# Middle stage of a hybrid decoder layer: low weight parts by accumulating transfers inside SBUF, and two more weight slots

## The chip, the cores and the metric

The kernel runs on one core of one Trainium2 chip, in float32 throughout. The metric is the device time of one execution in microseconds (us); three executions of the kernel before have a median of 1206.13 us.

## What is computed

One decoder layer for 512 prompt tokens and 32 sample tokens (8 sequences of 4), 544 columns in all, with the same weights:

```python
x = x + 0.5 * SwiGLU_1(RMSNorm(x))            # D_MODEL 1024, D_FF 2816
h = RMSNorm(x); z = h @ w_in                  # 1024 x 3584, split among head groups
x = x + concat(MoBA(q_a, k_a, v_a),           # 8 heads of 64, softmax attention
               gate * norm(HGRN2(q_b, f_b, i_b))) @ w_out   # 4 heads of 128, gated recurrence
x = x + 0.5 * SwiGLU_2(RMSNorm(x))
```

The prompt attends within itself; the samples attend to 1024 cached keys and values that are gathered by a page table (64 gathers of 512 KB). New keys, values and recurrent states are outputs too.

## The kernel before, in words

**Tiles and products.** Activations lie transposed, features on the 128 partitions and 544 tokens along the free dimension. A float32 product is made of three TensorE passes in float32r: weights and activations are each cut into a high part (the value rounded to float32r) and a low part (the rest), and high x high, high x low and low x high are added in PSUM (`products`, line 608). One output tile of a projection takes 8 row blocks x 2 column halves x 3 passes = 48 matmuls of 272 columns.

**Weights.** A weight matrix is worked off in jobs (`weight_jobs`, line 449), each of two "units" of up to 128x512 elements (256 KB). A unit is loaded by SyncE into one of four `raw` buffers (`w_load`), then split (`split_unit`, line 530): ScalarE copies it with rounding into `whi`, VectorE subtracts that from the raw tile into `wlo`. The pair lies in one of four weight slots (line 993). A projection takes two units (`next_w(2)` in `gemm`, line 618) and gives them back at its end (`free_w`), which calls `w_pump` (line 572): as long as fewer than AHEAD = 4 units are waiting, and a slot is free, the next unit is split; then as many loads are issued as raw buffers allow. With four slots and two in use, two units can lie ready ahead. The two FFNs use Strassen-like paired jobs for most of gate and up, which borrow six further slots; gate and up of the first five blocks, down, w_in and w_out are plain jobs.

**Stages.** FFN 1 (about 0 to 400 us); the mixer or middle stage (about 400 to 790 us: 28 projections from w_in, the attention of prompt and samples, the recurrence, two products with w_out); the other six products with w_out and FFN 2 (to the end). In the middle stage the projections are the backbone of TensorE's order, and chains of other work are woven into it: `pair_qk` (line 1142) norms a pair of key and query heads, with the tiles `kn` (high part by ScalarE, low part by VectorE), `qh`, `ql`, and a multiply of `kt` on GpSimd; `prompt_tile` does one tile of the prompt's softmax attention; `hgrn_head` one head of the recurrence; `sample_scores` and `sample_rest` read the gathered cache, tiles `KV`, five buffers. The chain of a sample's values (`sample_rest`) can begin only when all four value projections are done.

**What sets the order.** A planner (`Order`, line 254) runs the whole program once with modelled costs for each engine and for the DMA engines, and notes each instruction with its modelled start; the instructions are then given out in the order of these starts, so every engine's queue is fixed by the model. TensorE goes on with a due chain if there is one, and with the backbone otherwise. For a transfer the model takes 0.06 us of the issuing engine, 1.5 us of latency and the bytes at 330 KB a us (`Order.dma`, line 358); 1.0 us of GpSimd for an indirect gather. GpSimd issues the gathers and, at the end of the stage, eight reloads of x (`y<-xs`, line 1769). The queue of each engine is strictly in order: an instruction that waits holds back all behind it.

Before, line 534 is the only thing that makes a low part:

```python
hi, lo = self.take_slot(x, (F32R, F32R))
nc.scalar.copy(hi[:, :nk], src[:, :nk])
nc.vector.tensor_tensor(lo[:, :nk], src[:, :nk], hi[:, :nk].bitcast(F32), op=ALU.subtract)
```

Of the kernel before, what the change touches and what calls it, by code (L numbers as in the profile page):

```python
# [14 lines left out]
AF = mybir.ActivationFunctionType  # L15
ALU = mybir.AluOpType
# [5 lines left out]
KD = D // 128  # L22
# [19 lines left out]
COLS = {"qa": 0, "ka": 512, "va": 1024, "qb": 1536, "fb": 2048, "ib": 2560, "gb": 3072}  # L42
# [8 lines left out]
OVER, TICK, WARM_COLUMNS = 0.0112, 3.413, 3060  # L51
NREG = 5
AHEAD = 4
PACE = 0.8
WARM = 10
SLACK = -0.1
# [52 lines left out]
class View:  # L109
# [9 lines left out]
    def step(self, op, *args, **kw):  # L119
        return View(self.tensor, getattr(self.model, op)(*args, **kw), self.path + ((op, args, kw),))  # L120
# [58 lines left out]
class Engine:  # L179
# [22 lines left out]
    def __getattr__(self, op):  # L202
        real = getattr(self.real, op)

        def call(*args, **kw):
            names = list(self.tensors(args, kw))
            if op == "dma_start":
                s = self.order.dma(self.part, 4 * args[1].shape[0] * self.free(args[1]), names)
            elif op == "indirect_dma_start":
                s = self.order.dma(self.part, 4 * args[0].shape[0] * self.free(args[0]),  # L210
                                   names + [args[3].ap.tensor.name], 1.0)
            else:
                s = self.order.spend(self.part, self.cost(op, args, kw), names, op, self.shares_port(op, args, kw))
            self.order.note(s, real, args, kw)

        return call
# [37 lines left out]
class Order:  # L254
# [100 lines left out]
        for n in names:  # L355
            self.touched[n] = max(done, self.touched.get(n, 0.0))

    def dma(self, part, size, names, cost=0.06):
        s = self.fit(part, self.start(part, names), cost)
        e = self.fit("dma", s + cost + 1.5, size / 330e3) + size / 330e3  # L360
        self.finish(names, e, e + 0.3)
        return s

# [49 lines left out]
class Build:  # L413
# [35 lines left out]
    def weight_jobs(self):  # L449
        a, out = self.a, []  # L450

        def quarters(m, nk, r0, c0):
            h = nk // 2
            return [m[128 * r:128 * (r + h), c0:c0 + 128].rearrange("(k p) m -> p k m", p=128)
                    for r in (r0, r0 + h)]

        def plain(m, nk, r0, c0):
            out.append({"paired": False, "src": quarters(m, nk, r0, c0), "nk": nk // 2, "raw": [], "done": 0})

        def ffn(p):  # L460
            gate, up, down = (a[p + n][0] for n in ("_gate", "_up", "_down"))
            for g0, ng in FGROUPS:
                for f in range(g0, g0 + ng):
                    if f < NREG:
                        plain(gate, KD, 0, 128 * f)
                        plain(up, KD, 0, 128 * f)
                    else:
                        out.append({"paired": True, "nk": KD // 2, "raw": [], "done": 0,
                                    "src": quarters(gate, KD, 0, 128 * f) + quarters(up, KD, 0, 128 * f)})
                for m in range(KD):  # L470
                    plain(down, ng, g0, 128 * m)

        ffn("ffn1")
        for n, j in IN_ORDER:
            plain(a["w_in"][0], KD, 0, COLS[n] + 128 * j)
        for m in range(KD):
            plain(a["w_out"][0], KD, 0, 128 * m)
        ffn("ffn2")
        return out

# [46 lines left out]
            self.loading += 1  # L527
        return True

    def split_unit(self, src, nk, x):  # L530
        nc = self.nc
        hi, lo = self.take_slot(x, (F32R, F32R))
        nc.scalar.copy(hi[:, :nk], src[:, :nk])
        nc.vector.tensor_tensor(lo[:, :nk], src[:, :nk], hi[:, :nk].bitcast(F32), op=ALU.subtract)
        return hi, lo, x

    def w_split(self):
        if self.splitting == len(self.jobs):
            return False
        job = self.jobs[self.splitting]  # L540
        n = job["done"]
        if len(job["raw"]) <= (3 if job["paired"] else n):
            return False
        x = self.room("w", job)
        if x is None:
            return False
        nk = job["nk"]
        if job["paired"]:
            (a11, a12, a21, a22) = (r for r, _ in job["raw"])
            if n == 0:  # L550
                S = [self.tl(self.sums, [128, 4, 128], f"S{i}") for i in range(4)]
                for i, (e, p, q, op) in enumerate(((self.nc.vector, a21, a22, ALU.add),
                                                   (self.nc.vector, S[0], a11, ALU.subtract),
                                                   (self.nc.gpsimd, a11, a21, ALU.subtract),
                                                   (self.nc.gpsimd, a12, S[1], ALU.subtract))):
                    e.tensor_tensor(S[i][:, :nk], p[:, :nk], q[:, :nk], op=op)
                job["units"] = (a11, S[1], S[0], a12, S[2], S[3], a22)
            src = job["units"][n]
            self.units.append(self.split_unit(src, nk, x))
            drop = {0: (0, 2), 3: (1,), 6: (3,)}.get(n, ())  # L560
        else:
            self.units.append(self.split_unit(job["raw"][n][0], nk, x))
            drop = (n,)
        for i in drop:
            raw, y = job["raw"][i]
            self.release(y, raw)
        job["done"] += 1
        if job["done"] == (7 if job["paired"] else 2):
            self.splitting += 1
        return True  # L570

    def w_pump(self):
        while (len(self.units) < AHEAD and self.w_split()) or self.w_load():
            pass

    def next_w(self, n):
# [84 lines left out]
    def right_factors(self, pool, x, gain):  # L661
# [14 lines left out]
        for k in range(n):  # L676
# [12 lines left out]
            for step in steps:  # L689
                step()  # L690
                self.order.t = self.order.free["pe"] + PACE
                yield
# [278 lines left out]
    def load_x(self, pool, p, x):  # L971

        nc, a = self.nc, self.a
# [3 lines left out]
        s = p.tile([NS, D], F32, name="xins")  # L977
        nc.scalar.dma_start(s, a["x_sample"].rearrange("b t d -> (b t) d"))
        xin = {}
        src = a["x_prompt"][0].rearrange("(i p) d -> p i d", p=128)  # L980

        def load(c, n):
            t = p.tile([128, 4, n], F32, name=f"xin{c}")
            nc.sync.dma_start(t, src[:, :, c:c + n])
            for k in range(n // 128):
# [4 lines left out]
        self.units = []  # L990
        self.turn = False
        self.slots = {"raw": [{"pool": self.wp, "tags": ("raw",), "bufs": 4, "used": 0, "freed": [], "extra": None}],
                      "w": [{"pool": self.wp, "tags": ("whi", "wlo"), "bufs": 4, "used": 0, "freed": [], "extra": None}]}
        w = [self.first_weights() for _ in range(2)]
        load(0, 128)
        w[0][1](0)
# [50 lines left out]
        out = [self.tl(pool, [128, T], t, bufs=2) for t in ("t_s", "t_h")]  # L1047
# [797 lines left out]
```

## Time and profile before

| | |
|---|---|
| Median of three executions | 1206.13 us (1203.18 to 1208.79) |
| The profiled execution | 1210.65 us, its span 1208.9 us |
| TensorE busy | 1178.1 us, 97% of the span |
| VectorE, ScalarE, GpSimd busy | 858.5, 551.9, 228.3 us |
| Bytes moved | 144.74 MB, 120 GB/s on the mean |

How to read the rows further down. PE is TensorE's matmuls, PEld its weight loads, DVE VectorE, ACT ScalarE, POOL GpSimd, SPq the queue of SyncE. Every instruction of this kernel is recorded at line 284, where the planner gives it out, so the tiles' names tell the operations apart: `wlo<-raw,whi` reads raw and whi and writes wlo. A row of a table by stretches has the stretch in us, its length, busy us of PE, PEld, DVE, ACT and POOL (number of instructions in brackets), then the mean granted clock of TensorE (1.00 is 2.4 GHz, 0.50 is 1.2 GHz), the mean busy share of the 16 DMA engines, and GB/s. A row of a timeline has the start, the length, the engine, the operation and the tiles, the number of instructions merged into it, and in square brackets the idle time before it and what ended it. A row of groups has the count, the busy us and mean ns of one, then the idle time before them and what ended it. A row of waits says who waited for whom: us in total, times, the longest.

### The profile page before, as it was taken

Reading aid. Unit: us, or ns where it says so; the run is one execution under the profiler, and the core shown is the slowest. Engines: PE = TensorE matmul, PEld = TensorE weight load, DVE = VectorE, ACT = ScalarE, POOL = GpSimd, SP = SyncE. Lnnn points to the kernel's source line nnn. Section 1 sums busy time; section 2 is a strip of 40 time slices with the busy share of each in tenths; the row PEclk is TensorE's granted clock in tenths of the full one; section 3 lists DMA queues with packets and bytes.
Section 4 is the critical chain, followed back from the end, with each engine's and each line's share of the span. In section 5 each row is a group of like instructions: output and inputs, shape, how many; then the busy total and the mean of one; then the engine's idle time right before and its main releaser. Section 6 shows DMA issues by size and latency. Waiting matters only on the chain.

```text
span 1208.9 us, 26320 instructions
## 1 busy us (share of the span) xinstructions
PE 1178.1 (97%) x10571; PEld 1113.7 (92%) x10571; DVE 858.5 (71%) x1729; ACT 551.9 (46%) x1125; POOL 228.3 (19%) x211
## 2 busy tenths in 40 slices
PE   8999999999999999989999999899999999999998
PEld 8989999999999988878878867799999999999998
DVE  6988559954875698877776557667977488736843
ACT  6455246532654345554556433344554266524632
POOL 3012012200202401000332344220020023102200
PEclk9999999999999999989999999899999999999999
DMA  5244453333314642322565776352344323323222
GB/s 161 79 123 114 133 148 97 97 106 87 87 54 135 193 129 69 97 72 74 181 195 160 235 262 222 111 158 79 93 118 131 97 81 104 106 87 88 63 79 82
DMA packets 216238, 144.74 MB, mean 120 GB/s; under 512 B 12035, under 2 KB 204067, under 8 KB 216116
## 3 DMA queue, kind: packets, MB, share of 16 engines
q1 hardware_dynamic: 205588, 106.60, 30.6%
q0 software_dynamic: 10432, 36.32, 9.1%
q8 instruction: 83, 1.36, 0.5%
q14 instruction: 39, 0.32, 0.1%
q10 hardware_dynamic: 96, 0.14, 0.0%
HBM read 133.94 MB, written 11.83 MB: 121 GB/s over the span
## 4 chain that ended last, share of the span: by engine, by line
PE 77%; DVE 13%; ACT 3%; DMA 3%; issue 2%; SPq 1%; POOL 0%; DVEq 0%; ACTq 0%; POOLq 0%
PE mm L284 51%; PE sm L284 26%; DVE wlo L284 3%; DVE xl L284 2%; DVE xwl L284 1%; DMA raw<-ffn_down 1%; ACT xh L284 1%; DVE t_h L284 1%; SPq L284 1%; ACT whi L284 1%; DVE hl L284 1%; ACT sq L284 1%; DMA raw<-ffn_up 1%; DVE S L284 1%; DMA KV<-cache_v,idx 1%
## 5 line engine op out<-in xcount | busy, mean ns | idle before, releaser
L284 PE MATMUL mm<-xh,whi 128*128 128x272 f32 x1216 | 365.0, 300 | 1.0 <-DVE t_g L284 0.5
L284 PE MATMUL mm<-xl,whi 128*128 128x272 f32 x1216 | 352.4, 290 | 5.4 <-DVE xl L284 5.2
L284 PE MATMUL mm<-xh,wlo 128*128 128x272 f32 x1216 | 353.2, 290 | 1.1 <-DVE wlo L284 1.1
L284 ACT CAST whi<-raw 128x512 fp32r<-128x512 f32 (+1 forms) x230 | 138.7, 604 | 261.4 <-PE mm L284 192.3
L284 PEld LDWEIGHTS mm<-xh,whi 128*128 128x128 f32 x1216 | 231.5, 190 | 18.2 <-issue 15.7
L284 PEld LDWEIGHTS mm<-xl,whi 128*128 128x128 f32 x1216 | 231.3, 190 | 6.4 <-DVE xl L284 6.2
L284 PEld LDWEIGHTS mm<-xh,wlo 128*128 128x128 f32 x1216 | 231.0, 190 | 2.1 <-DVE wlo L284 2.1
L284 DVE TENSOR_TENSOR wlo<-raw,whi 128x512 fp32r<-128x512 f32 (+1 forms) x230 | 165.1, 727 | 81.0 <-ACT whi L284 77.4
L284 POOL TENSOR_TENSOR S<-raw,raw 128x512 f32<-128x512 f32 x18 | 30.4, 1691 | 380.9 <-DMA raw<-ffn_up 261.1
L284 PE MATMUL mm<-hh,whi 128*128 128x272 f32 x352 | 101.5, 288 | 0.3 <-DVE x L284 0.3
L284 PE MATMUL mm<-hh,wlo 128*128 128x272 f32 x352 | 101.1, 287 | 0.0
L284 PE MATMUL mm<-hl,whi 128*128 128x272 f32 x352 | 101.1, 287 | 0.0
L284 PE MATMUL mm<-xwh,xh 128*128 128x272 f32 x296 | 85.4, 288 | 1.3 <-DVE t_h L284 0.8
L284 PE MATMUL sm<-xwl,xh 128*128 128x272 f32 x296 | 85.3, 288 | 0.0
L284 PE MATMUL mm<-xwl,xh 128*128 128x272 f32 x296 | 85.3, 288 | 0.0
L284 PE MATMUL sm<-xwh,xh 128*128 128x272 f32 x296 | 85.2, 288 | 0.0
L284 PE MATMUL mm<-xwh,xl 128*128 128x272 f32 x296 | 85.2, 288 | 0.0
L284 PE MATMUL sm<-xwh,xl 128*128 128x272 f32 x296 | 85.2, 288 | 0.0
L284 DVE TENSOR_TENSOR xl<-S,xh 128x512 fp32r<-128x512 f32 x84 | 66.0, 796 | 4.1 <-ACT xh L284 3.7
L284 PEld LDWEIGHTS mm<-hh,whi 128*128 128x128 f32 x352 | 66.3, 188 | 0.7 <-ACT whi L284 0.5
L284 ACT CAST xh<-S 128x512 fp32r<-128x512 f32 x84 | 51.8, 620 | 32.7 <-DVE S L284 13.7
L284 PEld LDWEIGHTS mm<-hh,wlo 128*128 128x128 f32 x352 | 66.2, 188 | 0.0
(325 smaller groups left out, 2639.2 us busy)
## 6 DMA issues: line engine op xcount, KB each, us to landing
raw<-ffn_down SPq DMA_DIRECT2D x64, 256.0 KB
raw<-ffn_gate SPq DMA_DIRECT2D x56, 256.0 KB
raw<-ffn_up SPq DMA_DIRECT2D x56, 256.0 KB
raw<-w_in SPq DMA_DIRECT2D x56, 256.0 KB
raw<-ffn_down SPq DMA_DIRECT2D x32, 192.0 KB
xl<-ffn_gate SPq DMA_DIRECT2D x16, 256.0 KB
xh<-ffn_up SPq DMA_DIRECT2D x16, 256.0 KB
xl<-ffn_up SPq DMA_DIRECT2D x16, 256.0 KB
```

The source lines that it names most:

```text
L284: call(*map(real, args), **{k: real(v) for k, v in kw.items()})
```

## The change

For the jobs of w_in and w_out alone (marked "mixer"), VectorE's subtraction is replaced: ScalarE writes the negated, rounded copy of the raw tile into the low tile, and GpSimd issues a transfer inside SBUF that adds the raw tile onto it. For these jobs up to AHEAD_MIX = 6 units are split ahead instead of 4. The weight slots are six instead of four in every stage; the room for them comes from a descriptor scratch of 8192 bytes a partition. The planner takes 1.3 us of GpSimd for each direct transfer that it issues, the reloads of x too, and 3.0 us of latency for an accumulating one.

```diff
+AHEAD_MIX = 6
             if op == "dma_start":
-                s = self.order.dma(self.part, 4 * args[1].shape[0] * self.free(args[1]), names)
+                pool = self.part == "pool"
+                s = self.order.dma(self.part, 4 * args[1].shape[0] * self.free(args[1]), names,
+                                   1.3 if pool else 0.06, 3.0 if "accum_op" in kw else 1.5)
-    def dma(self, part, size, names, cost=0.06):
+    def dma(self, part, size, names, cost=0.06, latency=1.5):
         s = self.fit(part, self.start(part, names), cost)
-        e = self.fit("dma", s + cost + 1.5, size / 330e3) + size / 330e3
+        e = self.fit("dma", s + cost + latency, size / 330e3) + size / 330e3
         for n, j in IN_ORDER:
-            plain(a["w_in"][0], KD, 0, COLS[n] + 128 * j)
+            plain(a["w_in"][0], KD, 0, COLS[n] + 128 * j, True)
         for m in range(KD):
-            plain(a["w_out"][0], KD, 0, 128 * m)
+            plain(a["w_out"][0], KD, 0, 128 * m, True)
-    def split_unit(self, src, nk, x):
+    def split_unit(self, src, nk, x, transfer=False):
         nc = self.nc
         hi, lo = self.take_slot(x, (F32R, F32R))
         nc.scalar.copy(hi[:, :nk], src[:, :nk])
+        if transfer:
+            nc.scalar.activation(lo[:, :nk], src[:, :nk], AF.Identity, scale=-1.0)
+            nc.gpsimd.dma_start(lo[:, :nk], src[:, :nk], accum_op=ALU.add)
+            return hi, lo, x
         nc.vector.tensor_tensor(lo[:, :nk], src[:, :nk], hi[:, :nk].bitcast(F32), op=ALU.subtract)
         return hi, lo, x
-            self.units.append(self.split_unit(job["raw"][n][0], nk, x))
+            self.units.append(self.split_unit(job["raw"][n][0], nk, x, job["mixer"]))
     def w_pump(self):
-        while (len(self.units) < AHEAD and self.w_split()) or self.w_load():
+        def ahead():
+            mixer = self.splitting < len(self.jobs) and self.jobs[self.splitting]["mixer"]
+            return len(self.units) < (AHEAD_MIX if mixer else AHEAD)
+
+        while (ahead() and self.w_split()) or self.w_load():
             pass
-                      "w": [{"pool": self.wp, "tags": ("whi", "wlo"), "bufs": 4, "used": 0, "freed": [], "extra": None}]}
+                      "w": [{"pool": self.wp, "tags": ("whi", "wlo"), "bufs": 6, "used": 0, "freed": [], "extra": None}]}
-    nc = bacc.Bacc("TRN2", target_bir_lowering=False, num_devices=1)
+    nc = bacc.Bacc("TRN2", target_bir_lowering=False, num_devices=1, dynamic_dma_scratch_size=8192)
```

## Rows read from the trace of the kernel before

**Rows 1.** The page: span, and busy time and share of each engine.
```profile
span 1208.9 us, 26320 instructions
PE 1178.1 (97%) x10571; PEld 1113.7 (92%) x10571; DVE 858.5 (71%) x1729; ACT 551.9 (46%) x1125; POOL 228.3 (19%) x211
```

**Rows 2.** Table by stretches: plain products, and the stage of the prompt's attention.
```profile
410.00:420.00 10.00, 10.00 (x82) 10.00 (x81) 3.70 (x7) 3.04 (x6) 7.19 (x12) 1.00 0.68 191
430.00:560.00 130.00, 124.78 (x998) 108.43 (x1000) 108.54 (x282) 65.21 (x158) 9.41 (x9) 0.95 0.29 83
```

**Rows 3.** Table by stretches: the two places at which the clock fell.
```profile
495.00:505.00 10.00, 9.34 (x52) 8.09 (x51) 8.74 (x23) 5.23 (x13) 0.87 (x1) 0.83 0.29 82
530.00:545.00 15.00, 11.98 (x53) 9.71 (x53) 10.83 (x30) 6.51 (x18) 0.04 (x1) 0.66 0.25 70
```

**Rows 4.** Table by stretches: the value gathers, and the end of the mixer.
```profile
700.00:728.00 28.00, 27.35 (x406) 18.97 (x407) 15.53 (x42) 8.46 (x24) 15.19 (x16) 1.00 0.78 270
738.00:762.00 24.00, 21.74 (x424) 15.33 (x416) 14.85 (x41) 4.08 (x12) 14.59 (x14) 1.00 0.77 254
762.00:780.00 18.00, 12.51 (x132) 10.97 (x128) 13.47 (x37) 6.48 (x20) 0.00 (x0) 0.81 0.18 55
```

**Rows 5.** Timeline of VectorE: pairs of low-part splits, and the steps of kn.
```profile
448.40 1.28 DVE L284 TENSOR_TENSOR wlo<-raw,whi 128x512 fp32r<-128x512 f32 x2
...
493.76 2.65 DVE L284 TENSOR_TENSOR wlo<-raw,whi 128x512 fp32r<-128x512 f32 x2
...
496.45 0.75 DVE L284 SCALAR_TENSOR_TENSOR kn<-sm,qkg,kn 64x512 fp32r<-64x512 f32 x1
...
527.95 2.65 DVE L284 TENSOR_TENSOR wlo<-raw,whi 128x512 fp32r<-128x512 f32 x2
...
530.62 0.74 DVE L284 SCALAR_TENSOR_TENSOR kn<-sm,qkg,kn 64x512 fp32r<-64x512 f32 x1
```

**Rows 6.** Timeline of ScalarE: its steps of kn ahead of those.
```profile
493.75 0.68 ACT L284 ACTIVATE kn<-sm,qkg 64x512 fp32r<-64x512 f32 x1 [0.69 <-PE sm L284]
...
528.07 0.68 ACT L284 ACTIVATE kn<-sm,qkg 64x512 fp32r<-64x512 f32 x1 [0.92 <-PE sm L284]
```

**Rows 7.** Timeline of GpSimd at the same two times.
```profile
493.96 1.91 POOL L284 TENSOR_TENSOR kt<-kt,gkrow 128x640 f32<-128x640 f32 x1 [23.44 <-issue]
528.28 1.77 POOL L284 TENSOR_TENSOR kt<-kt,gkrow 128x640 f32<-128x640 f32 x1 [32.41 <-PE sm L284]
```

**Rows 8.** TensorE's waits from 440 to 560 us.
```profile
PE sm L284 <- DVE kn L284: 4.1, 3, 3.2
```

**Rows 9.** Groups of VectorE from 400 to 790 us: the low-part splits.
```profile
L284 DVE TENSOR_TENSOR wlo<-raw,whi 128x512 fp32r<-128x512 f32 x60 | 45.1, 768 | 14.7 <-ACT whi L284 14.1
```

**Rows 10.** Timeline of VectorE in the tail of the mixer: one split.
```profile
765.09 0.69 DVE L284 TENSOR_TENSOR wlo<-raw,whi 128x512 fp32r<-128x512 f32 x1
```

**Rows 11.** TensorE's waits over the whole span: those for low parts.
```profile
PE mm L284 <- DVE wlo L284: 1.1, 2, 0.6
```

**Rows 12.** Groups of ScalarE from 400 to 790 us: the high parts, and a scaled copy.
```profile
L284 ACT CAST whi<-raw 128x512 fp32r<-128x512 f32 x60 | 37.1, 619 | 55.6 <-PE mm L284 45.6 <-issue 6.9 <-PE sm L284 1.8
...
L284 ACT ACTIVATE qn<-z,qkg 128x544 f32<-128x544 f32 x4 | 3.0, 755 | 0.5 <-DVE z L284 0.5
```

**Rows 13.** Groups of GpSimd over the span: an indirect and a direct transfer.
```profile
L284 POOL DMA_INDIRECT KV<-cache_v,idx x32 | 31.5, 984 | 43.5 <-PE sm L284 40.0 <-issue 1.2 <-PE mm L284 0.8
...
L284 POOL DMA_DIRECT2D y<-xs x8 | 4.4, 580 | 22.2 <-PE mm L284 22.2
```

**Rows 14.** GpSimd's waits from 690 to 770 us.
```profile
POOL KV L284 <- PE sm L284: 37.8, 23, 11.2
```

**Rows 15.** The page's DMA queues: packets, MB, share of 16 engines.
```profile
q0 software_dynamic: 10432, 36.32, 9.1%
```

**Rows 16.** Timelines of GpSimd and VectorE: the reloads of x and their first use.
```profile
782.70 4.39 POOL L284 DMA_DIRECT2D y<-xs  x8 [22.20 <-PE mm L284]
...
788.43 0.79 DVE L284 TENSOR_TENSOR y<-mm,y 128x272 f32<-128x272 f32 x2 [0.23 <-DMA y<-xs]
```

More of the change, by code (lines that the diff above doesn't have):

```diff
@@ L455, in quarters, with plain @@
                     for r in (r0, r0 + h)]
-        def plain(m, nk, r0, c0):
-            out.append({"paired": False, "src": quarters(m, nk, r0, c0), "nk": nk // 2, "raw": [], "done": 0})
+        def plain(m, nk, r0, c0, mixer=False):
+            out.append({"paired": False, "src": quarters(m, nk, r0, c0), "nk": nk // 2, "raw": [], "done": 0,
+                        "mixer": mixer})
         def ffn(p):
@@ L467, in ffn @@
                     else:
-                        out.append({"paired": True, "nk": KD // 2, "raw": [], "done": 0,
+                        out.append({"paired": True, "nk": KD // 2, "raw": [], "done": 0, "mixer": False,
                                     "src": quarters(gate, KD, 0, 128 * f) + quarters(up, KD, 0, 128 * f)})
```

## The prediction, made before the changed kernel was run

> **What bounds the kernel now.** First the busy shares [rows 1]: TensorE is busy 1178.1 of 1208.9 us, so all that any change of the weight splits can give back is some 31 us of TensorE idle time and the time in which its clock is halved. Then the table by stretches: where is TensorE not full? In a stretch of plain products it starts 82 matmuls in 10 us, 0.122 us each. From 430 to 560 us, the stage of the prompt's attention, it is idle 5.2 of 130 us while VectorE is busy 108.5 [rows 2]. Most of that is two places [rows 3]. From 495 to 505 us TensorE is idle 0.66 us and the granted clock is 0.83: after the pause it ran 3.4 us at 1.2 GHz, 1.7 us of lost work. From 530 to 545 us it is idle 3.02 us at a clock of 0.66: 10.2 us at 1.2 GHz, 7.2 of them busy, 3.6 us lost. So the two places cost 2.4 and 6.6 us. A third is the end of the mixer, 762 to 780 us: 5.5 us idle at a clock of 0.81 [rows 4].
>
> What ends the wait? The timelines of VectorE and ScalarE say it [rows 5, 6]. Both times a pair of key heads is being normed: ScalarE finishes the high part kn at 494.43 and 528.75 us, but VectorE takes up its step of kn only at 496.45 and 530.62, because two low-part splits (wlo, 2.65 us together) stand in front of it. Both pairs run beside GpSimd's kt multiply [rows 7]; a pair without it took 1.28 us [rows 5]. TensorE's products of kn come after that: 4.1 us of waits, one of 3.2 [rows 8]. So VectorE's queue, and the weight splits in it, set the end here, and they are what the change takes away.
>
> **The change part by part.** (1) *VectorE loses its part of 72 units* (56 of w_in, 16 of w_out; 60 of them between 400 and 790 us, 768 ns each, 45.1 us [rows 9]). Most of that lies beside a full TensorE and is worth nothing. On the path are: the first stall, where kn moves up by 496.45 - 494.43 = 2.0 us, more than the 0.66 us of idle time, so the idle time and the fall of the clock go: 2.4 us. The second stall, where kn moves up by 1.87 us: 1.2 us of idle time stays, since further ScalarE and VectorE steps of the same chain follow, and I let half of the clock's loss stay with it: 1.87 + 1.8 = 3.7 us (between 1.9, if the clock falls all the same, and 6.6). The other 1.5 us of idle time from 430 to 560 (5.2 - 0.66 - 3.02): taken by half, 0.7 us (0 to 1.5). In the tail one wlo of 0.69 us stands between the steps of a root that the last head needs [rows 10]: 0.7 us. What is late next in the two stalls is the turn-taking of ScalarE and VectorE on one tile.
>
> (2) *Two more slots, everywhere.* In the two FFNs the limit stays four units, but with six slots two more can be split while two are in use. TensorE's waits for wlo there are 1.1 us in all [rows 11]: I take them whole, 1.1 us (0 to 1.1).
>
> (3) *ScalarE gets the negated copy*: 72 instructions that the trace does not show. Nearest rows: the cast of the same tile, 619 ns, and an activation with a scale on 128x544, 755 ns, or 710 at 512 columns [rows 12]. So 72 x 0.62 to 0.71 = 45 to 51 us on an engine that was busy 552 of 1209 us [rows 1]. Before kn it waited 0.69 and 0.92 us for TensorE [rows 6], so one more copy in front fits there. But some will stand ahead of a softmax or norm step: I charge 1.0 us (0 to 4, if six of them lie bare).
>
> (4) *GpSimd issues 72 transfers*, not in the trace. Nearest: a direct load took 580 ns (4.4 us for eight), an indirect gather 984 [rows 13]: 42 to 71 us on an engine busy for 228. A transfer waits in GpSimd's queue for its negated copy; behind it stand the cache gathers and the kt and state multiplies. The reverse holds too: a transfer can stand behind a gather that waits for a buffer, up to 11.2 us [rows 14]. The cover is GpSimd's idle time and the lead (6).
>
> (5) *72 x 256 KB through the DMA engines.* The software queue moved 36.32 MB in 9.1% of the span [rows 15], 110 us of all 16 engines, 330 KB a us, so 0.79 us a unit; if the target is read as well, 1.6 us. I take 0.79, the nearest row, and keep both ends. In most of the stage this is covered. The place where it may not be is the value gathers, 700 to 728 and 738 to 762 us, with DMA shares of 0.78 and 0.77 [rows 4]: room for 6.2 + 5.5 us. I expect six to eight units between 700 and 780 us; at 0.79 us they need 6.3 us at most, and fit, but a gather in whose way one stands lands later: 1.5 us (0 to 13, see B).
>
> The Trainium skill (DMA: Bandwidth & Descriptors, Rules for kernel authors) says that an accumulating transfer reads its destination and writes it later, and (same page, Issuing engines are not separate DMA queues) that the transfers of all issuers interleave on the same 16 engines. By that I estimate 1.6 us a unit, and the sum below would be some 1 to 5 us worse. No row here shows an accumulating transfer.
>
> (6) *The low part comes later.* Before: a cast, then 0.7 us. After: cast 0.62, negated copy 0.7, issue 0.6, landing. For the landing the nearest row is the first of eight reloads of x: issued at 782.70 us, used at 788.43 after a wait for it [rows 16]: 5.7 us with seven others behind it; from below the 0.8 of the data alone. So 3 to 8 us from raw to low part. The lead is now two projections, four units beside the two in use: 2 x 48 matmuls x 0.122 us = 11.7 us (before 5.9). It covers this, unless the transfer stands behind a gather of 11.2 us. Cost 0.
>
> (7) *The planner* hands out every queue's order by modelled times. It now sees VectorE freer, transfers from GpSimd at 1.3 us and landings of 3.0 us, so TensorE's own order in the middle stage changes. The same products are issued; which stall comes where is not in the trace. I put 0, and 4 us to either side.
>
> Sum: gained 2.4 + 3.7 + 0.7 + 0.7 + 1.1 = 8.6; paid 1.0 + 1.5 = 2.5; net 6.1 us. The profiled execution took 1210.65 us (span 1208.9), so it would become 1204.5. The median of the runs shown is 4.5 us lower, 1206.13, and no term depends on that difference: **1200.0 us**, 0.5% faster.
>
> **The rivals.** *A: the wait moves, the end does not (no change).* VectorE is relieved, but the chain of a pair is then held by ScalarE, which has one more instruction for each unit, and by the turns between the engines. For it: the steps of kn go from ScalarE to VectorE and back. Then only the bare idle time of the stalls comes back, 0.66 + 1.87 = 2.5 us, less 1.0 for ScalarE: 1.5 us, **1204.6**. Against it: from 430 to 560 us ScalarE is busy 65 us against VectorE's 108.5 [rows 2]; 23 units at 0.65 bring it to 80.
>
> *B: the value gathers wait (slower).* From 700 us on the gathers and TensorE's use of five buffers run as one chain, and the end of the mixer hangs on its last buffer. If a unit costs this chain its issue (0.6 to 1.0) and 1.6 us of DMA, 2.4 us, eight units cost 19.2 us; less the 7.6 us that the other terms give (8.6 - 1.0), the kernel is 11.6 us slower: **1217.7**. It decides from about 1.0 us a unit on the chain (8 units = 7.6 us) and is over 0.5% slower from 1.7. For it: from 762 us TensorE has little else to do [rows 4]. Against it: the DMA room of 11.7 us. A second road to the same side: a transfer caught behind an 11.2 us gather wait arrives after 11.2 + 5 us against a lead of 11.7; 4.5 us of idle time, and as much again by the clock. Twice is 18 us, less the 6.1: 1218.
>
> *C: the change gives more.* The whole 9.0 us of the two stalls and 5.5 us of the tail go, since chains that no longer queue on VectorE all end sooner: 1206.1 - 14.5 + 2.5 = **1194**.
>
> **How the numbers follow.** Forecast 0.29 and C 0.13 (the faster side, 0.42); A 0.35; B 0.23. About 0.5%, 6.0 us, is what a measurement of this kernel can tell from no change: faster is below 1200.1, slower above 1212.2. Faster 0.42, same 0.35, slower 0.23. The forecast's own range is 1195 to 1204 (the second stall at its ends, the planner's 4 us in part). The range for 8 in 10 takes in A and C with 2 us beyond, and of B what lies below 1213: **1192 to 1213**.
>
> **What would show it.** Right: no wlo on VectorE from 400 to 790 us; VectorE from 430 to 560 us down from 108 by some 18 us; TensorE's waits for kn (4.1 us) below 2; no stretch of the middle at a clock near 0.5. A: these waits as long, with ScalarE named. B: from 700 us gathers spaced wider, TensorE waiting for KV, a longer tail, or TensorE waiting for wlo with a DMA as releaser. An issue far from 0.6 to 1.0 us on GpSimd, or landings over 8 us, would make steps 4 to 6 wrong.

## The result and the profile after

The changed kernel took 1216.47 us (median; 1213.94 to 1218.02), the kernel before on the same chip 1205.22 us (1203.18 to 1208.79): a ratio of 1.0087, 95% interval 1.0065 to 1.0110. It is slower, by some 11 us, where 6 us less was forecast, and above the range. Run once more on another chip (after_again, below) the same kernel gave 1.0101.

The profiled execution took 1213.94 us, its span is 1212.2 us. It is the fastest of its five, and the profiled execution of before, 1210.65 us, lies above all the times listed for that kernel, so the two profiles differ by 3.3 us only. The second profiled execution of the changed kernel has a span of 1218.4 us, near its median. Both are used.

The page of the changed kernel: busy times, the software queue (packets, MB, share of 16 engines), the new issues with their time to landing, and their group (count, busy us and mean ns, idle time before).

```profile
span 1212.2 us, 26433 instructions
PE 1176.2 (97%) x10571; PEld 1112.8 (92%) x10571; DVE 804.1 (66%) x1657; ACT 588.5 (49%) x1197; POOL 295.1 (24%) x283
...
q0 software_dynamic: 20800, 55.19, 18.0%
...
wlo<-raw POOLq DMA_DIRECT2D x72, 256.0 KB, 4.7
...
L287 POOL DMA_DIRECT2D wlo<-raw x72 | 65.4, 943 | 137.0 <-ACT wlo L287 132.2
```

VectorE gave up 54 us and GpSimd took 67 more than in [rows 1]. The software queue went from 9.1% [rows 15] to 18.0%: 18.0% of 1212.2 less 9.1% of 1208.9 is 108 us, 1.50 us of all 16 engines for each of the 72 units.

The stretches of [rows 2 to 4] again, and the end of the mixer in steps of 5 us (busy PE, PEld, DVE, ACT, POOL; clock; DMA share; GB/s):

```profile
430.00:560.00 130.00, 125.63 (x1159) 109.68 (x1158) 102.86 (x283) 78.97 (x185) 40.11 (x48) 0.99 0.69 161
495.00:505.00 10.00, 10.00 (x82) 9.66 (x81) 9.03 (x26) 8.39 (x15) 3.57 (x4) 1.00 0.91 205
530.00:545.00 15.00, 14.45 (x108) 12.06 (x107) 10.74 (x31) 9.23 (x22) 4.18 (x4) 1.00 0.53 123
738.00:762.00 24.00, 24.00 (x500) 18.70 (x500) 17.32 (x45) 10.71 (x32) 17.79 (x17) 1.00 0.95 285
762.00:780.00 18.00, 13.50 (x125) 11.55 (x125) 11.15 (x31) 4.29 (x7) 0.00 (x0) 0.91 0.30 96
785.00:790.00 5.00, 1.20 (x10) 0.98 (x8) 0.00 (x0) 0.00 (x0) 4.47 (x8) 0.93 1.06 247
790.00:795.00 5.00, 2.46 (x11) 2.46 (x12) 2.02 (x5) 1.30 (x2) 0.54 (x1) 0.50 0.96 330
```

The last two of these stretches in the kernel before:

```profile
785.00:790.00 5.00, 5.00 (x43) 5.00 (x42) 2.31 (x5) 1.87 (x3) 2.09 (x4) 1.00 1.05 342
790.00:795.00 5.00, 5.00 (x42) 5.00 (x41) 3.55 (x7) 3.85 (x8) 1.41 (x1) 1.00 0.89 273
```

The two stalls of [rows 3] are gone: TensorE is full or nearly so, at a clock of 1.00. The value gathers, where rival B put its price, run beside a full TensorE (738 to 762). But from 785 to 795 us, where it was full before, TensorE is idle for 6.3 of 10 us, and then at half its clock. And over the whole stretch from 430 to 560 us it is idle 4.4 us against 5.2 before: a new stall has come, the wait of 3.3 us for hqh in the next rows. What TensorE waited for, over the whole span:

```profile
PE mm L287 <- DVE y L287: 6.9, 2, 6.3
PE mm L287 <- DVE xl L287: 4.7, 4, 3.0
PE sm L287 <- DVE hqh L287: 3.3, 1, 3.3
PE mm L287 <- DVE wlo L287: 2.1, 4, 1.2
```

The 4.1 us of waits for kn [rows 8] are no longer among them. The longest wait is new: for y, the first addition onto the reloaded x. GpSimd's and VectorE's timelines show why:

```profile
780.04 0.99 POOL L287 DMA_DIRECT2D wlo<-raw  x1 [18.40 <-ACT wlo L287]
...
784.83 0.85 POOL L287 DMA_DIRECT2D wlo<-raw  x1 [0.19 <-issue]
786.11 3.79 POOL L287 DMA_DIRECT2D y<-xs  x7 [0.43 <-issue]
790.53 0.54 POOL L287 DMA_DIRECT2D y<-xs  x1 [0.64 <-DMA wlo<-raw]
...
792.04 0.79 DVE L287 TENSOR_TENSOR y<-mm,y 128x272 f32<-128x272 f32 x2 [15.13 <-DMA y<-xs]
```

Four transfers of w_out's units stand in front of the reloads, and the first three of them waited for ScalarE's negated copy (18.40, 0.52 and 1.35 us). ScalarE in its turn stood waiting for TensorE in front of these splits. The first seven reloads then wait for nothing else ("issue" ends the idle time before them), the eighth for the landing of a transfer. Before, they were issued at 782.70 us, when TensorE released them, and used at 788.43 [rows 16].

The second new wait, for xl, is 27 us into the kernel, in FFN 1, which the change was not meant to touch. VectorE's timeline and the table's row for 20 to 30 us, first in the kernel before, then in the changed one:

```profile
20.39 3.09 DVE L284 SCALAR_TENSOR_TENSOR xl<-x,gains,xh 128x544 fp32r<-128x544 f32 x2
26.82 1.29 DVE L284 TENSOR_TENSOR wlo<-raw,whi 128x512 fp32r<-128x512 f32 x2
...
35.72 0.69 DVE L284 COPY R<-sm 128x512 f32<-128x512 f32 x1 [0.68 <-PE sm L284]
...
20.00:30.00 10.00, 10.00 (x81) 10.00 (x81) 7.30 (x10) 5.78 (x11) 6.01 (x5) 1.00 0.12 33
```

```profile
20.70 1.29 DVE L287 SCALAR_TENSOR_TENSOR xl<-x,gains,xh 128x544 fp32r<-128x544 f32 x1
21.91 3.60 DVE L287 TENSOR_TENSOR wlo<-raw,whi 128x512 fp32r<-128x512 f32 x2
25.44 1.85 DVE L287 SCALAR_TENSOR_TENSOR xl<-x,gains,xh 128x544 fp32r<-128x544 f32 x1
...
39.69 0.69 DVE L287 COPY R<-sm 128x512 f32<-128x512 f32 x1 [1.31 <-PE sm L287]
...
20.00:30.00 10.00, 6.99 (x49) 6.77 (x48) 7.98 (x8) 5.75 (x12) 6.56 (x5) 0.91 0.18 52
```

The two extra slots are free at the start, so two more units are split at once, and their 3.60 us on VectorE stand in front of an xl for which TensorE waits 3.0 us. By the copy of R, a later step, the changed kernel is 4.0 us behind; the rest of what FFN 1 loses comes after it and was not traced to a place.

**Where the time lies.** Five segments of the span, read from timelines: FFN 1, up to the first copy of a w_in projection out of PSUM; the prompt's attention, up to the first transposition of a gathered key; the cache, up to the last product with gathered values; the turn, up to the first addition onto the reloaded x; the rest. Microseconds, one profiled execution each.

| kernel | FFN 1 | attention | cache | turn | rest | span |
|---|---|---|---|---|---|---|
| before | 408.1 | 165.1 | 192.3 | 22.9 | 420.5 | 1208.9 |
| after, first | 415.3 | 157.5 | 194.3 | 24.9 | 420.2 | 1212.2 |
| after, second | 416.5 | 161.8 | 195.0 | 24.9 | 420.2 | 1218.4 |
| slots6_alone | 412.8 | 161.5 | 192.4 | 21.3 | 418.2 | 1206.2 |
| four_in_ffn | 408.1 | 160.4 | 196.8 | 25.6 | 420.8 | 1211.7 |
| no_transfer | 414.4 | 154.5 | 196.8 | 14.0 | 423.3 | 1203.0 |
| all_small | 414.6 | 158.0 | 195.6 | 23.6 | 420.6 | 1212.4 |
| out_small | 415.4 | 158.8 | 197.0 | 23.0 | 420.4 | 1214.6 |
| reload_sync | 415.4 | 159.2 | 198.3 | 27.1 | 420.2 | 1220.1 |
| reload_act | 413.6 | 160.2 | 194.7 | 21.4 | 426.0 | 1215.9 |
| w_in_only | 413.8 | 159.9 | 192.7 | 22.9 | 418.9 | 1208.2 |
| w_in_four | 409.0 | 157.3 | 196.9 | 21.3 | 418.9 | 1203.4 |
| w_in_four, again | 409.2 | 160.0 | 194.5 | 21.4 | 419.0 | 1204.1 |
| lead_four | 408.0 | 161.0 | 192.0 | 21.8 | 419.8 | 1202.6 |

The two executions of one and the same kernel differ by 4.3 us in the attention, so a difference of that size between two rows says nothing there. Up to the first splits of the mixer's weights, some 20 us before the end of FFN 1, every engine's queue is in the same order in all kernels with six slots there, and their nine executions take 412.8 to 416.5 us; the five with four slots take 408.0 to 409.2. The rows also come from several chips, on which the medians of the kernel before run from 1205.22 to 1210.19 us: spans are not compared across rows, only stages, and times by ratio. Against before, the changed kernel loses 7.2 to 8.4 us in FFN 1, 2.0 to 2.7 in the cache stage and 2.0 in the turn, and gains 3.3 to 7.6 in the attention.

### The profile page after: what moved, and what is told of

Its sections match the earlier page's. It is cut to its first block, busy times and chain, and to the rows that moved or that the text cites. A ratio compares the mean times of both kernels' runs of the same rounds, so it can differ in the third digit from the quotient of the medians.

```text
span 1212.2 us, 26433 instructions
## 1 busy us (share of the span) xinstructions
PE 1176.2 (97%) x10571; PEld 1112.8 (92%) x10571; DVE 804.1 (66%) x1657; ACT 588.5 (49%) x1197; POOL 295.1 (24%) x283
## 4 chain that ended last, share of the span: by engine, by line
PE 75%; DVE 8%; DMA 6%; issue 5%; ACT 3%; POOL 3%; SPq 0%; POOLq 0%; ACTq 0%; DVEq 0%
PE mm L287 50%; PE sm L287 25%; DMA KV<-cache_v,idx 2%; DVE xl L287 2%; POOL KV L287 1%; DVE wlo L287 1%; DMA raw<-w_in 1%; DVE xwl L287 1%; DMA raw<-ffn_gate 1%; DMA raw<-ffn_up 1%; ACT whi L287 1%; DMA SC<-rsample 1%; DMA xin<-x_prompt 1%; POOL wlo L287 1%; DVE S L287 0%
## 5 line engine op out<-in xcount | busy, mean ns | idle before, releaser
L287 PEld LDWEIGHTS mm<-xh,whi 128*128 128x128 f32 x1216 | 231.3, 190 | 26.8 <-issue 14.7
L287 DVE TENSOR_TENSOR wlo<-raw,whi 128x512 fp32r<-128x512 f32 (+1 forms) x160 | 111.8, 706 | 46.0 <-ACT whi L287 43.2
L287 POOL TENSOR_TENSOR S<-raw,raw 128x512 f32<-128x512 f32 x18 | 27.4, 1522 | 341.2 <-DMA raw<-ffn_up 210.3
L287 POOL DMA_DIRECT2D wlo<-raw x72 | 65.4, 943 | 137.0 <-ACT wlo L287 132.2
L287 PE MATMUL mm<-xwh,xh 128*128 128x272 f32 x260 | 75.5, 290 | 1.9 <-DVE t_h L287 1.3
L287 PE MATMUL sm<-xwh,xl 128*128 128x272 f32 x260 | 75.0, 288 | 0.0
L287 PE MATMUL mm<-xwl,xh 128*128 128x272 f32 x260 | 75.0, 288 | 0.0
L287 PE MATMUL sm<-xwh,xh 128*128 128x272 f32 x260 | 75.0, 288 | 0.0
L287 PE MATMUL mm<-xwh,xl 128*128 128x272 f32 x260 | 75.0, 288 | 0.0
L287 PE MATMUL sm<-xwl,xh 128*128 128x272 f32 x260 | 74.9, 288 | 0.0
L287 PEld LDWEIGHTS mm<-hl,whi 128*128 128x128 f32 x352 | 66.2, 188 | 0.0
## 6 DMA issues: line engine op xcount, KB each, us to landing
raw<-ffn_down SPq DMA_DIRECT2D x32, 192.0 KB, 2.5
```

Source lines behind the costliest of these rows:

```text
L287: call(*map(real, args), **{k: real(v) for k, v in kw.items()})
```

## The experiments

All ratios are to the kernel before on the same chip, with a 95% interval. Diffs are against the changed kernel where nothing else is said.

### Which part of the change costs

**slots6_alone**: the kernel before with six slots and the scratch.

```diff
-  "tags": ("whi", "wlo"), "bufs": 4,
+  "tags": ("whi", "wlo"), "bufs": 6,
-  nc = bacc.Bacc("TRN2", target_bir_lowering=False, num_devices=1)
+  nc = bacc.Bacc("TRN2", target_bir_lowering=False, num_devices=1, dynamic_dma_scratch_size=8192)
```

> The kernel before with six weight slots (and the smaller scratch that makes room for them), and nothing else: low parts on VectorE everywhere, four units ahead. Theory 1 (the two extra slots let splits run in front of FFN 1's first activations): the start is some 4 us later, the first projection's first evacuation near 415 us instead of 408, the whole 4 to 8 us slower than before, 1209 to 1213. Theory 2 (all of the loss is the load of the transfers on the DMA engines): within 2 us of before, 1203 to 1207.

Measured 0.9990 (0.9972 to 1.0007). In total that is theory 2's, but not because the slots do nothing: FFN 1 is 4.7 us longer, as theory 1 said, and the attention 3.6 (within what two executions of one kernel differ by), the turn 1.6 and the rest 2.3 us shorter. A price and a gain of about the same size cancel.

**four_in_ffn**: the jobs of the FFNs keep to four slots; the mixer has six.

```diff
- free = [x for x in self.slots[kind] if x["used"] < x["bufs"] and ...
+ free = [x for x in self.slots[kind]
+         if x["used"] < (x["bufs"] if x["extra"] is not None or job["mixer"] or kind == "raw" else 4) and ...
```

> The changed kernel, but jobs of the FFNs may hold only four of the six slots; the mixer's may hold all six. Theory 1: FFN 1 is as before (first evacuation of a projection near 408 us), 5 to 8 us faster than the changed kernel, 1208 to 1212. Theory 2: as the changed kernel, 1214 to 1218.

Measured 1.0021 (1.0004 to 1.0037), some 0.7% better than the changed kernel's 1.0087 and 1.0101. FFN 1 takes 408.1 us, as before. VectorE's timeline and TensorE's row at the place shown above:

```profile
19.73 3.09 DVE L287 SCALAR_TENSOR_TENSOR xl<-x,gains,xh 128x544 fp32r<-128x544 f32 x2
26.15 1.29 DVE L287 TENSOR_TENSOR wlo<-raw,whi 128x512 fp32r<-128x512 f32 x2
...
35.06 0.69 DVE L287 COPY R<-sm 128x512 f32<-128x512 f32 x1
...
20.00:30.00 10.00, 10.00 (x82) 10.00 (x81) 6.65 (x9) 4.66 (x9) 5.34 (x5) 1.00 0.18 52
```

The xl come ahead of the splits again, TensorE is full, and the copy of R, 4.6 us later in the changed kernel, is back. So the slots' price in FFN 1 is shown: without it 8 to 10 of the 11 to 12 us that the changed kernel loses against before are back. The next run gets all of them back, and more, in another way, so these shares do not add up to the loss.

**no_transfer**: the transfers are planned but not issued.

```diff
- self.order.note(s, real, args, kw)
+ if "accum_op" not in kw:
+     self.order.note(s, real, args, kw)
```

> The changed kernel with the 72 accumulating transfers planned as before but not issued: the low part is left as the negated high part, so this part of the computation is left out. Every other queue keeps its instructions and order. Theory 1: what the transfers cost is the value gathers and the reloads of x, 4 to 7 us: 1209 to 1213, FFN 1 as late as in the changed kernel. Theory 2: the transfers are all of the loss, 11 us or more: at or below 1205.

Measured 0.9967 (0.9951 to 0.9982): with neither VectorE nor transfers making the low parts, six slots and all, the kernel is 0.3% faster than before and some 1.3% (15 us) faster than the changed one. That is what issuing the 72 transfers costs, against low parts that come from nowhere. It is theory 2's number, with theory 1's late FFN 1 (414.4 us) still in it. The turn shrinks to 14.0 us; GpSimd's timeline:

```profile
776.13 4.39 POOL L288 DMA_DIRECT2D y<-xs  x8 [15.79 <-DVE xl L288]
```

The cache stage stays long (196.8), though no transfer runs in it. So in this run what the stage lost comes from the new plan or from ScalarE's copies, not from gathers that a transfer delays.

**w_in_only**: transfers for w_in alone, w_out's 16 units on VectorE.

```diff
- plain(a["w_out"][0], KD, 0, 128 * m, True)
+ plain(a["w_out"][0], KD, 0, 128 * m)
```

> The changed kernel once more, unaltered, so that the three runs beside it have its time on the same chip. Both theories expect its first ratio, 1.009 of the kernel before, within 0.002.

> The changed kernel with transfers for the 56 units of w_in alone; the 16 units of w_out get their low part on VectorE again. Six slots stay. Theory P (the price is paid at the end of the mixer, where the eight reloads of x stand behind w_out's transfers): from the last value product to the first add on the reloaded x it takes 24.9 us after the change and 14.0 with no transfer sent; here 14 to 18, so 7 to 11 us faster than the changed kernel, 0.999 to 1.003 of the kernel before. Rival Q (the price is the DMA traffic and GpSimd's issues anywhere in the mixer, 108 us of all 16 engines for 72 units): 56 of 72 units stay, so only 16/72 of the 10.1 us that lie between the changed kernel and the one with no transfer come back, 2.3 us, 1.007.

Measured 1.0101 (1.0083 to 1.0119) for the changed kernel again, and 1.0027 (1.0009 to 1.0045) here: 8.3 us of median back by 16 of the 72 units. The total is theory P's, and rules Q out. Where P placed it is only partly right: the turn fell from 24.9 to 22.9 us, not to 14 to 18. TensorE's wait of 6.3 us for y is gone, but the reloads are issued at 783.95 us, 17.5 us after the last value product (18.9 in the changed kernel, 17.2 before). With no transfer in front they wait for TensorE, as before, and the 14.0 us of no_transfer, on which P built, hold only where low parts come from nowhere. In the profiles FFN 1, where the two kernels do not differ, gives 2.7, the attention 1.9 and the cache stage 2.3 us of the rest, no more than what executions of one kernel differ by.

### Queue or data

**reload_sync** and **reload_act**: the eight reloads of x issued by SyncE, or by ScalarE.

```diff
- nc.gpsimd.dma_start(x[k], xspill[k])
+ nc.sync.dma_start(x[k], xspill[k])      # reload_act: nc.scalar
```

> The changed kernel with the eight reloads of x issued by SyncE instead of GpSimd, so that they no longer stand behind the transfers of w_out's units. Theory 1: the 6.3 us wait of TensorE for y shrinks by 2 to 4 us; 1212 to 1215. Theory 2 (DMA load): the reloads land as late as before, 1215 to 1218.

> The changed kernel with the eight reloads of x issued by ScalarE. They no longer stand behind w_out's transfers in GpSimd's queue, nor behind the weight loads of SyncE's, but the transfers still move their 1.5 us each through the same DMA engines beside them. If the place in GpSimd's queue is what makes them late: issued by about 777 us (776.1 with no transfer), the first add on the reloaded x at 780 to 785 us in place of 792, and 7 to 10 us faster than the changed kernel. If the DMA load is what makes them late: issued earlier, but landing as late as before, within 3 us of the changed kernel's time.

Measured 1.0094 (1.0068 to 1.0121) and 1.0091 (1.0073 to 1.0109): neither helps. With SyncE TensorE's wait for y grew to 8.2 us. SyncE's queue with its waits from 780 to 800 us, and ScalarE's queue:

```profile
789.55 6.99 SPq L287 DMA_DIRECT2D raw<-w_out  x4
796.82 4.05 SPq L287 DMA_DIRECT2D y<-xs  x8
...
SPq L287 <- DMA wlo<-raw: 18.7, 4, 13.4
```

```profile
785.78 12.00 ACTq L287 DMA_DIRECT2D y<-xs  x7
797.83 0.75 ACT L287 ACTIVATE xh<-y,gains 128x544 fp32r<-128x544 f32 x1 [11.60 <-DMA y<-xs]
```

On SyncE they stand behind loads of w_out that wait for raw buffers, and these are held until a transfer has read them. On ScalarE the first comes at 785.39 us, behind the copies of the same w_out units, the last at 797.3, and what the turn gains (21.4 us) is lost in the rest (426.0). Every queue has something in front that hangs on w_out's splits, so these two do not tell queue from data. The next two do.

**all_small** and **out_small**: every issue and wait stays, each transfer moves 128x32 elements only.

```diff
+ if "accum_op" in kw and kw.pop("small"):
+     args = [x[:, :1, :32] for x in args]
  self.order.note(s, real, args, kw)
...
- nc.gpsimd.dma_start(lo[:, :nk], src[:, :nk], accum_op=ALU.add)
+ nc.gpsimd.dma_start(lo[:, :nk], src[:, :nk], accum_op=ALU.add, small=True)   # out_small: for w_out's jobs
```

> The changed kernel with each of the 72 transfers cut from 128x512 to 128x32 elements (16 KB in place of 256): every issue, every wait and the plan stay, the data all but go. It leaves the low part of the other columns as the negated high part. So the 1.0095 of the changed kernel is split: if GpSimd's queue (issue of 0.94 us and what stands behind it) is the price, 1.006 to 1.010; if the DMA traffic is (1.5 us of all 16 engines a unit), near the 0.997 of the kernel with no transfer sent, at most 1.001.

> The same cut for the 16 units of w_out alone (their low part stays the negated high part but for 32 columns); the 56 of w_in are moved whole. If the reloads of x are late because w_out's transfers load the DMA engines: as the run with w_in's units alone, 1.003 (1.001 to 1.005), first add on the reloaded x some 18 to 21 us after the last value product. If they are late because they stand behind the transfers in GpSimd's queue: 1.008 to 1.010 and 24 to 25 us.

Measured 1.0024 (1.0008 to 1.0039) and 1.0057 (1.0037 to 1.0077): both between the two expectations. Of the transfers' 1.3%, about 0.7 goes with the data and 0.6 (1.0024 against 0.9967) stays with issues and waits. For w_out's 16 units alone, 0.3 to 0.4% goes with the data (1.0057 against 1.0087 and 1.0101) and 0.3 stays (against w_in_only's 1.0027). The cut is not a clean one: the software queue's share is 11.2% of 1212.4 us here, still 0.36 us of all 16 engines for a transfer of 16 KB. What stays is the queue in front of the reloads, in all_small (GpSimd's timeline, TensorE's wait):

```profile
786.35 0.85 POOL L289 DMA_DIRECT2D wlo<-raw  x1 [0.19 <-issue]
787.62 4.32 POOL L289 DMA_DIRECT2D y<-xs  x8 [0.43 <-issue]
...
PE mm L289 <- DVE y L289: 4.5, 1, 4.5
```

The reloads still come 19.4 us after the last value product. Part of what the data costs shows at 430 to 456 us. The table's row for 430 to 450 us before; then ScalarE, VectorE and TensorE in after_again, and its row:

```profile
430.00:450.00 20.00, 19.55 (x229) 18.25 (x230) 17.79 (x48) 10.15 (x20) 2.63 (x2) 1.00 0.19 54
...
449.72 0.62 ACT L287 CAST whi<-raw 128x512 fp32r<-128x512 f32 x1 [5.62 <-DMA raw<-w_in]
...
451.39 1.01 DVE L287 TENSOR_REDUCE ms_qk<-sq 128x8 f32<-128x512 f32 x2 [3.73 <-ACT sq L287]
...
456.94 0.74 PE L287 MATMUL sm<-fc,kt 128*128 128x128 f32 x5 [4.17 <-DVE kt L287]
...
430.00:450.00 20.00, 18.32 (x332) 16.98 (x331) 16.10 (x43) 5.27 (x10) 13.39 (x19) 1.00 1.00 274
```

and the same split and the same row in all_small:

```profile
446.68 0.62 ACT L289 CAST whi<-raw 128x512 fp32r<-128x512 f32 x1 [2.17 <-issue]
...
430.00:450.00 20.00, 17.20 (x304) 15.46 (x303) 15.14 (x44) 6.81 (x14) 10.21 (x12) 0.91 0.62 192
```

Transfers, the five gathers of the first keys and values (at 436 to 442 us here, at 416 to 421 before), and the weight loads fill the DMA engines: a share of 1.00, against 0.19 before and 0.62 with the small transfers. A load of w_in lands late, ScalarE stands 5.6 us in front of its high part, the norm step sq behind it waits, and with it ms_qk, kt and TensorE: 4.2 us. ScalarE's waits for loads of w_in from 415 to 560 us are 14.7 us in this execution, 9.2 in the first (longest 4.1, and no TensorE wait for kt). With the small transfers, and before, there is none to be listed. That a late load can stop the norm chain is a rival I did not have. In the first execution TensorE loses 3.3 us at the same place on another path: GpSimd waits 4.1 us for the load of rsample and comes late to clearing hs, VectorE waits 2.2 us for hs, and TensorE 3.3 us for hqh; in all_small these waits are 2.2 us, none and 0.9. That the full DMA engines are the cause there too was not tried by itself. Such waits do not always reach TensorE: w_in_four, below, has 10.5 and 8.6 us of the same waits of ScalarE and is faster than before. From 425 to 462 us TensorE is idle 5.9 us in after_again, 3.3 in the first execution, 2.8 in all_small and 2.2 before. So this place holds 0.5 to 3 us of the 8 that go with the data and the turn 1.3 (24.9 against 23.6 us); the profiles do not place the rest.

### A version that is faster, and why

**w_in_four**: w_in_only and four_in_ffn together, run twice. **lead_four**: its control, no transfer at all.

```diff
# lead_four: four_in_ffn, and
- if transfer:
+ if False:        # every low part by VectorE's subtraction, six units ahead in the mixer
```

> As the run with w_in's units alone, and the jobs of the two FFNs keep to four slots, so that their splits run no further ahead than in the kernel before. Theory P: the first FFN's projection starts at 408 us as before (415 with six slots in the FFN), and some of these 7 us last to the end, as 2.4 us did where only this was changed: 0.994 to 1.000 of the kernel before, the first version that is not slower than it. Rival Q: 1.004 to 1.006.

> The changed kernel with all 72 low parts on VectorE, six units ahead in the mixer, four slots in the FFNs: all of the change but the transfers and the slots' price in the first FFN. The control for w_in_four (0.998). If taking the low parts off VectorE is what makes w_in_four faster than before: 1.000 to 1.002 here, the stalls of the prompt's attention back (5 us and more of idle time from 430 to 560 us). If the two extra units of lead alone do it: 0.996 to 0.998.

> The version with w_in's units alone and four slots in the FFNs once more, beside its control on the same chip: 0.998 of the kernel before, within 0.002.

Measured: w_in_four 0.9979 (0.9964 to 0.9995) and, on a second chip, 0.9952 (0.9930 to 0.9973); lead_four beside the latter 0.9954 (0.9936 to 0.9973), 1205.28 against 1210.19 us. Both values of that chip lie a little below what the runs expected (0.996 at the lowest). So the faster version owes nothing that can be measured to the transfers: six slots and six units ahead in the mixer give its 0.5% without them. The planner's price for the reloads is in lead_four too, and the three were not separated; slots6_alone, with four units ahead, already has nearly the same attention and turn (161.5 and 21.3 us against 161.0 and 21.8). lead_four in the stretches of [rows 2, 3], TensorE's wait for kn, and VectorE at the second pair:

```profile
430.00:560.00 130.00, 127.22 (x1051) 111.56 (x1050) 109.55 (x293) 66.09 (x161) 9.40 (x9) 0.96 0.29 83
530.00:545.00 15.00, 14.81 (x90) 12.19 (x90) 12.08 (x34) 6.63 (x17) 1.90 (x1) 0.89 0.36 106
495.00:505.00 10.00, 9.44 (x55) 8.29 (x55) 9.22 (x21) 5.63 (x13) 1.26 (x1) 0.87 0.56 159
...
PE sm L287 <- DVE kn L287: 1.0, 3, 0.5
...
528.80 1.28 DVE L287 TENSOR_TENSOR wlo<-raw,whi 128x512 fp32r<-128x512 f32 x2
...
532.33 1.53 DVE L287 SCALAR_TENSOR_TENSOR kn<-sm,qkg,kn 64x512 fp32r<-64x512 f32 x2 [0.36 <-ACT kn L287]
```

VectorE is as busy as before (109.55 against 108.54 us), yet TensorE is idle 2.8 us in place of 5.2. At the second pair the splits come 3.5 us ahead of kn instead of right in front of it, and TensorE's waits for kn in the whole stretch fall from 4.1 to 1.0 us. So at the second pair it was not VectorE's load that made the stall, but which two splits stood where. At the first pair little changed: in lead_four too two splits end right in front of kn, and TensorE is idle 0.56 us from 495 to 505 us against 0.66.

**The ladder** that the ratios make: lead_four 0.9954; with w_in's transfers 0.9952 and 0.9979; with w_out's as well (four_in_ffn) 1.0021, 5 to 8 us more; with six slots in the FFNs too (the changed kernel) 1.0087 and 1.0101, 8 to 10 us more. The shares hold for this order of steps: with the slots left in, taking the transfers out gave 15 us (no_transfer).

## Why the prediction was wrong

**Step 2 failed, and by the ladder it weighs most.** The two slots "everywhere" were put at a gain of 1.1 us. In FFN 1 they cost 7.2 to 8.4 us. I read TensorE's waits for wlo there, which a slot can only shorten, and did not ask what a free slot lets VectorE do at the start, when TensorE is not yet held by the weights but by xl. The limit of four units ahead does not hold this back: it counts units that wait, and the four units of the first two products are never among them, so the fifth and sixth are split as soon as slots are free. That alone turns the sum of -6.1 us into +2 to +3. In medians (four_in_ffn) it is 8 to 10 us. That the slots alone (slots6_alone, 0.9990) came out near the 1.1 us forecast is luck: the gain was expected from waits for wlo in the FFNs, but FFN 1 paid 4.7 us, and the stages behind it gave them back.

**Steps 4 and 5 failed too: together they were put at 1.5 us, and the list of what is queued behind a transfer was incomplete.** Issuing the transfers costs 15 us against none sent, and 8 us (0.9954 to 1.0021) against low parts on VectorE with the same slots. I named the gathers and the kt and state multiplies, and not the eight reloads of x, though they stood in [rows 16] and were used there as a price. The turn is 2.0 us longer than before for it, with a TensorE wait of 6.3 us and, behind it, 5 us at a clock of 0.50, which the prediction's own signs had excluded for the middle stage; with four slots in the FFNs, w_out's transfers cost 5 to 8 us of the median. The issue cost 943 ns, at the upper end of the 0.58 to 0.98 given.

**Step 5's size:** 1.50 us a unit, not the 0.79 that I took. The Trainium skill (DMA: Bandwidth & Descriptors, Rules for kernel authors) says that an accumulating transfer reads its destination. The trace agrees with the estimate made from that, 1.6 us. The place was wrong too: not at the value gathers, but in part at the first gathers, from 430 to 456 us, and in the turn.

**Step 1 was right on its place, and roughly on its size.** The stalls at 495 to 505 and 530 to 545 us went as said, the waits for kn with them. The attention is 3.3 to 7.6 us shorter, forecast 6.8 with the rest of the stretch. But the cause was only half seen: lead_four, with every split still on VectorE, removes three quarters of the wait for kn and has an attention 4.1 us shorter. VectorE from 430 to 560 us fell by 6 us, not 18: the stretch holds 1159 matmul records of TensorE instead of 998, and as many instructions of VectorE as before (283 and 282) though none is a split, so more of VectorE's other work fell into it.

**Step 3:** 627 ns for a negated copy, between the two rows given. Its price on the path was not measured by itself.

**Step 6 held:** landings took 4.7 us (3.3 to 8.0), and no wait of TensorE had one of these transfers as its releaser.

**Step 7** stays open. In all profiled executions with the transfers in the plan, no_transfer too, the cache stage takes 192.7 to 198.3 us, against 192.0 to 192.4 in the three without. Whether that is the order of the plan or ScalarE's copies was not tried.

**Rivals.** B gave a time close to what came, 1217.7, by a mechanism that is not there: TensorE waited 1.4 us for gathered tiles after 560 us (before 1.7), and the cache stage is as long with no transfer sent. A fell, the chain of a pair was not held by ScalarE. C fell: at the end of the mixer, from 762 to 780 us, TensorE is still idle 4.5 us (before 5.5). I had no rival for a part of the change outside the stage that the change is for.

## What to carry to other kernels

A buffer pool that is enlarged for one stage is enlarged for all: ask of each stage what will be done earlier than before, and in front of what it then stands. When work is moved to another queue, write out everything that this queue issues until the end of the stage, the reloads for the next stage included, and ask of each whether it can now wait on the moved work's own inputs. And before moving work off an engine whose queue stands in front of a critical step, try the control that only moves it in time: here the longer lead, with the slots that it needs, gave 0.5%, and the transfers added nothing to it that could be measured.

## What the hardware showed that was not expected

An accumulating transfer of 256 KB inside SBUF cost 1.50 us of all 16 DMA engines, beside weight loads and gathers, about twice what the same bytes took on average in the software queue of before (0.79 us); cut to a sixteenth of the data it still cost 0.36 us. GpSimd spent 943 ns on the issue (918 for the small one), and landing took 4.7 us in the median.

Two splits on VectorE took 3.60 us at 21.91 us in the changed kernel, beside two of GpSimd's additions of squares (from 21.5 and 23.3 us, 1.7 us each), and 1.29 us at 26.15 us in four_in_ffn, after the last of these. So work brought forward by a free slot did not only come first, it was also 2.8 times as long.
